# One decoder layer on one core: the first loads, the first norm, the gate rows and the planner's price for scans are changed

## The chip, the cores and the metric

The kernel runs on one core of one Trainium2 chip. The metric is the device time of one execution in microseconds, the median of several runs. The kernel before took 1553.03 us (three runs, 1550.15 to 1555.63).

## What is computed

One layer of a hybrid decoder, for a prompt of 256 tokens and 8 single-token samples together (N = 264 columns), width 2048, all in float32. Cut to what matters here:

```python
xn = rmsnorm(x, g_mix)                       # the "first norm"
z = xn @ w_in                                # RG-LRU input and gate, q, k, v, o, and 4 + 4 gate columns i, f
xr, conv_new = causal_conv(z_rgx, conv_buf, conv_w, conv_b)
r  = sigmoid(block_diag(xr, w_rg_a, b_rg_a))
ig = sigmoid(block_diag(xr, w_rg_x, b_rg_x))
log_a = -8 * r * softplus(-lam)
a  = exp(log_a)
bx = sqrt(max(1 - exp(2 * log_a), 0)) * ig * xr
h_t = a_t * h_{t-1} + bx_t                   # RG-LRU, a scan over the tokens
y_rg = rmsnorm(h * gelu(z_rgg), g_rg_out)
logi, logf = z_i + b_i, log_sigmoid(z_f + b_f)
h_ml, C, n, m = mlstm(q, k, v, logi, logf, C0, n0, m0)   # 4 heads, running maximum as stabiliser
y_ml = rmsnorm(h_ml, g_ml_out) * sigmoid(z_o)
x = x + concat(y_rg, y_ml) @ w_out
x = x + cross_attention(rmsnorm(x, g_xa), memory)
x = x + swiglu(rmsnorm(x, g_ffn))
y = rmsnorm(x, g_final)
```

The outputs are y, the recurrent states of both groups and the memory keys and values.

## The kernel before

**Layout.** The residual `xres` holds the 2048 features as 16 chunks of 128 partitions by 264 columns. Each product with a weight block of 128 by 128 is made of three fp32r products, high x high, high x low and low x high (`mm3`): ACT copies a float32 tile into a rounded high part, DVE subtracts it from the original for the low part (`split` for activations, `split_half` and `split_first` for weights). A float32 matmul that isn't split shows as two records in the profile.

**Steps.** `steps` is a list of weight pieces in order, each with its PE work and an evacuation function. A piece of 128 x 2048 feeds 48 products (16 chunks x 3) of 264 columns into one PSUM bank. Steps 0 to 3 compute the first four output blocks of `w_in` together, 4 of the 16 chunks of x in each step ("pieces" c of 512 columns, 16 in all), into four banks. Steps 4 to 7 are the other four RG-LRU input blocks, step 8 the gate columns, 9 to 16 q and k, 17 to 24 v, 25 to 32 the RG-LRU gate, 33 to 40 the mLSTM output gate, from 41 on `w_out`, then cross-attention and the feed-forward.

**Buffers.** Raw weight halves have 5 buffers, split weight halves (`w`) have 4, which is two steps' worth: the halves of step n + 2 reuse those of step n. PSUM has 4 banks `mm`, for the steps, and 4 banks `ax`, for everything else; a step's bank is the one of four steps before and has to be evacuated by then. Small temporaries `t` have 6 buffers.

**Order.** Weights are loaded on SP's queue, whose order is the order of the program text. On PE, DVE and ACT the framework's scheduler orders the instructions by priority with a timeline of its own, except inside `in_order()` (ACT and DVE) or another `manual_schedule`, where the program order holds. Once built, every engine executes its instructions strictly in the built order, and waits for what the instruction at its head needs. Work beside the steps (first norm, scans, gates, mLSTM, its norm) is written as generators (`Gen`, `side`). After each step `pump` emits pieces of them as long as the planner's clocks of DVE and ACT stay below PE's; these clocks add up prices per instruction (`price_dve`, `price_act`, `price_pe`, lines 63 to 79). A generator of negative priority is emitted whole; `finish` emits until a condition holds; `need` names what has to be finished before a step.

**Start.** Lines 1280 to 1296: SP loads chunk 0 of x, then the weight pieces 0 to 3; ACT's queue loads the first 16 columns of small vectors and chunks 1 to 3 of x. PE first runs 12 products of `ones` (`warm(12)`, line 299).

**First norm.** The products of steps 0 to 3 use x times the gain, without the norm's factor; that factor, `rstd`, is applied when a bank is evacuated. During steps 1 to 3 `sumsq` squares the chunks of x on ACT and adds them up on DVE in `acc_x`. `norm_x` (through `rstd_from`, line 343) then sums over the partitions on PE (`token_sums`: windows of 128 columns of `acc_x` as the stationary operand, one column of ones as the moving one), computes the reciprocal root on DVE, and spreads it over all partitions on PE (`spread`), from where ACT copies it to `rstd`. It is emitted after step 3 and has to be finished before step 5; the evacuation of the first four banks follows. The generator of the RG-LRU (`rg_gen`) starts at step 5 too; it has a sigmoid stage, then 16 exponentials and 8 square roots on ACT (each function set needs a table load) and 8 scans on DVE.

**Gates.** `evac_if` and `ml_gates` work on 4 partitions, one for each head, in tiles `R(j)[0:4]`. Two scans on DVE give the cumulative sums and maxima. Four products with a contraction of 4 rows spread 16 values per head over the partitions; five transposes of 4 rows turn the rows into columns. `ml_prompt` (line 661) spreads the running maximum in the same way, in one product for each head.

**What sets the order around the change.** In the sum: an ACT split of a weight half waits until PE has left that buffer two steps before; the DVE subtraction waits for ACT; whatever stands behind that subtraction in DVE's built order waits too; and PE waits for whichever of these its next instruction needs.

Of the kernel before, what the change touches and what calls it, by code (L numbers as in the profile page):

```python
# [17 lines left out]
P = 128  # L18
D = 2048
KC = D // P  # L20
T = 256
# [42 lines left out]
def price_dve(name, n, a, k):  # L64
    fast = name in ("tensor_scalar", "tensor_copy", "tensor_single_scalar", "memset")
    if name == "tensor_reduce":
        n = int(np.prod(a[1].shape[1:]))
    return 0.07 + n * (0.00052 if fast else 0.0066 if name == "reciprocal" else 0.00104)


def price_act(name, n, a, k):
# [9 lines left out]
def layer_kernel(ctx: ExitStack, tc, xT, memT, vec, wrg, w_in, w_out, w_q, w_k, w_v, w_o,  # L81
# [150 lines left out]
    def mm3(ps, a, b, start, stop):  # L232
        ah, al = a
        bh, bl = b
        pe.matmul(ps, ah, bh, start=start, stop=False)
        pe.matmul(ps, ah, bl, start=False, stop=False)
        pe.matmul(ps, al, bh, start=False, stop=stop)

    st = {}
# [53 lines left out]
    def warm(n, w=None):  # L293

        ps = bank()
        for _ in range(n):
            pe.matmul(ps[:, :P], ones if w is None else w.to_broadcast([P, P]), ones, start=True, stop=True)

    warm(12)
    onesr = const.tile([P, P], F32R, name="onesr")  # L300
    mask = const.tile([P, P], F32, name="mask")
    pool_e.affine_select(out=mask, in_=ones, pattern=[[1, P]], compare_op=OP.is_ge, fill=0.0,
# [25 lines left out]

    WIN = (0, P, N - P)

    def token_sums(ps, acc, o=0, step=1):

        for j, w0 in enumerate(WIN if acc.shape[-1] == N else WIN[:2]):
            pe.matmul(ps[:, o + j * step: o + j * step + 1], acc[:, w0: w0 + P], ones[:, 0:1],
                      start=True, stop=True)

    def spread(ps, c, n=N):

# [236 lines left out]
    def evac_if(ps):  # L575
        R = Arr(7)
        ml["R"] = R
        li, u, a, b = (R(j)[0:4] for j in range(4))
        act.activation(a, ps[64:68, :N], AF.Copy)
        act.activation(b, ps[96:100, :N], AF.Copy)  # L580
        dve.tensor_add(li, ps[0:4, :N], a)
        dve.tensor_add(u, ps[32:36, :N], b)
        dve.tensor_mul(li, li, rstd[0:4, :])
        dve.tensor_mul(u, u, rstd[0:4, :])
        dve.tensor_scalar(li, li, V("bi")[0:4], None, op0=OP.add)
        dve.tensor_scalar(u, u, V("bf")[0:4], None, op0=OP.add)
        ml["gates"] = side(ml_gates(), 1)
# [6 lines left out]
    def ml_gates():  # L594
        R = ml["R"]
        li, u, e, lf, b, g, M = (R(j)[0:4] for j in range(7))
        yield STEP
        dve.scalar_tensor_tensor(e, u, -1.0, u, op0=OP.mult, op1=OP.min)
        act.activation(e, e, AF.Exp)
        yield 0.4  # L600
        log1p(lf, e)
        yield 6.0
        dve.tensor_scalar(u, u, 0.0, None, op0=OP.min)
        dve.tensor_sub(lf, u, lf)

        one = ones[0:4, 0:1].to_broadcast([4, T])
        dve.tensor_tensor_scan(b[:, :T], one, lf[:, :T], 0.0, op0=OP.mult, op1=OP.add)
        dve.tensor_sub(g[:, :T], li[:, :T], b[:, :T])
        dve.tensor_tensor_scan(M[:, :T], g[:, :T], g[:, :T], 0.0, op0=OP.max, op1=OP.max)
        dve.tensor_add(b[:, :T], b[:, :T], M[:, :T])  # L610
        dve.tensor_scalar(M[:, :T], M[:, :T], -1.0, None, op0=OP.mult)
        dve.tensor_copy(mrow[:, 0:1], b[:, T - 1: T])

        s = slice(T, N)
        dve.tensor_add(lf[:, s], lf[:, s], V("m0", 0, 8)[0:4])
        dve.tensor_max(b[:, s], lf[:, s], li[:, s])
        dve.tensor_copy(mrow[:, 1:], b[:, s])
        x16 = e[:, 0:16]
        dve.tensor_sub(x16[:, 0:8], lf[:, s], b[:, s])
        dve.tensor_sub(x16[:, 8:16], li[:, s], b[:, s])  # L620
        act.activation(x16, x16, AF.Exp)
        pool_e.dma_start(o_m, mrow)
        yield 3.0
        yield STEP
        yield STEP
        ps = bank("ax")
        for h in range(H):
            pe.matmul(ps[:, h * 16: h * 16 + 16], ident[0:4, h: h + 1].to_broadcast([4, P]), x16,
                      start=True, stop=True)
        i4 = ident[0:4, 0:4]  # L630
        for j in range(2):
            pe.transpose(ps[:, 64 + 4 * j: 68 + 4 * j], g[:, j * P: j * P + P], i4)
        for j, w0 in enumerate(WIN):
            pe.transpose(ps[:, 72 + 4 * j: 76 + 4 * j], b[:, w0: w0 + P], i4)
        act.activation(bcs, ps[:, 0:64].rearrange("p (h j) -> p h j", j=16), AF.Copy)
        act.activation(gcol, ps[:, 64:72].rearrange("p (j h) -> p j h", h=H), AF.Copy)
        act.activation(emc, ps[:, 72:84], AF.Exp, scale=-1.0)
        yield 0.1
# [26 lines left out]
    def ml_prompt():  # L665
        qk = ml["qk"]
        yield STEP
        kt = B([P, 2, H, P])
        for tb in range(2):
            ps = bank("ax")  # L670
            for h in range(H):
                pe.transpose(ps[:, h * P: h * P + P], qk(4 + h)[:, tb * P: tb * P + P], ident)
            act.activation(kt[:, tb].rearrange("p h d -> p (h d)"), ps, AF.Copy)
            yield STEP
        while "gates" not in ml or not ml["gates"].done:
            yield STEP
        R = ml["R"]
        M = R(6)[0:4, :T]
        for h in range(H):
            sel = ident[0:4, h: h + 1].to_broadcast([4, P])  # L680
            bc = bank("ax")
            pe.matmul(bc[:, :T], sel, M, start=True, stop=True)
            sps = bank("ax")
            q, k = qk(h), qk(4 + h)
            pe.matmul(sps[:, 0:256], k[:, 0:P], q[:, 0:T], start=True, stop=True)
            pe.matmul(sps[:, 256:384], k[:, P:T], q[:, P:T], start=True, stop=True)
            w = B([P, 1024])
            E, Pm, kw = w[:, 0:384], w[:, 384:768], w[:, 768:1024]
            ml["w", h] = (Pm, kw)
            yield STEP  # L690
            dve.tensor_scalar(E[:, 0:256], bc[:, 0:T], gcol[:, 0, h: h + 1], 0.0, op0=OP.add, op1=OP.min)
            dve.tensor_scalar(E[:, 256:384], bc[:, P:T], gcol[:, 1, h: h + 1], 0.0, op0=OP.add, op1=OP.min)
            act.activation(E, E, AF.Exp)
            dve.tensor_mul(E[:, 0:128], E[:, 0:128], mask)
            dve.tensor_mul(E[:, 256:384], E[:, 256:384], mask)
            dve.tensor_mul(Pm, sps[:, 0:384], E)
            act.activation(kw[:, 0:P], kt[:, 0, h, :], AF.Copy, scale=E[:, 255:256])
            act.activation(kw[:, P:T], kt[:, 1, h, :], AF.Copy, scale=E[:, 383:384])
            yield 1.0
            ml["pn"] = h + 1  # L700
# [167 lines left out]
    def proj(src, rhs, evac, cols=2048, n=N, need=()):  # L868

        def f(i):  # L870
            ps = bank()
            w = W(i)
            nch = cols // P
            for c in range(nch):
                mm3(ps[:, :n], w(c), rhs(c), c == 0, c == nch - 1)
            return ps
        steps.append((src, cols, f, evac, need))
# [399 lines left out]
    def load_x(e, lo, hi):  # L1277
        e.dma_start(xres[:, lo:hi, :], xT[:, lo:hi, :])  # L1278

    load_x(sp, 0, 1)  # L1280
    for c in range(4):
        load_first(0, c)
    for i in range(1, 3):
        for c in range(0, 4, 2):
            load_x(sp, 4 * i + c, 4 * i + c + 2)
            load_first(i, c)
            load_first(i, c + 1)
        if i == 1:
            sp.dma_start(vecs[:, 16:], vec[:, 16:])
    with tc.high_priority(), in_order():  # L1290
        act.dma_start(vecs[:, 0:16], vec[:, 0:16])
        load_x(act, 1, 2)
        load_x(act, 2, 4)
        act.activation(warm_act, ones[:, 0:1], AF.Square)
        split_half(0, 0)
        split_half(0, 1)

    pend = []
    for i, (src, cols, pef, evf, need) in enumerate(steps):
        if i > 1:  # L1300
            load_piece(i + LD - 1)
        if i == 5:
            finish(lambda: fn.done)
            st["rg"] = side(rg_gen(), 0)
        for q in need:
            if q in st:
                finish(lambda: st[q].done)
        if i != 4:
            with tc.high_priority(300):
                for e, x in pend:  # L1310
                    e(x)
            pend = []
# [2 lines left out]
        split_half(i + LS, 0)  # L1315
        if i + LS < len(steps) and steps[i + LS][1] > 1024:
            split_half(i + LS, 1)
        ps = pef(i)
        if 1 <= i < 4:
            with tc.issue_after(st["split"].ins):  # L1320
                for c in range(4 * i if i > 1 else 0, 4 * i + 4):
                    sumsq(acc_x, xres[:, c, :], c == 0)
        if i == 3:
            fn = side(norm_x(), -1)
        if evf is not None:
            pend.append((evf, ps))
        if i == 0:
# [124 lines left out]
```

## Time and profile before

| | |
|---|---|
| runs | 1550.15, 1553.03, 1555.63 us |
| the profiled execution | span 1548.1 us; it has no other time of its own |
| TensorE clock granted | 0.997 on average |
| instructions of PE | 12098 |
| read from memory | 312.78 MB, 209 GB/s over the span |
| chain that ended last | PE 96%, DVE 2%, ACT 1% |

A row of a timeline has the start and the length in us, engine, line, operation, tiles (output <- inputs, buffer numbers left out), shapes and count, and in brackets the idle time before it and who ended it. Line 60 is the wrapper through which all priced engine calls go, so tiles tell the calls apart: `mm` and `ax` are PSUM banks, `raw` and `w` weight halves before and after the split, `B` large tiles, `c` and `t` small ones. PEld is the loading of the stationary operand. In the chain of waits a row is start, length and what ran. A row of waits is: who waited for whom, us in total, times, longest. A row of windows has the window, its length, the busy time of PE, PEld, DVE, ACT and POOL with counts, the granted clock, the DMA share and GB/s.

### The profile page before, as it was taken

The numbers are of one execution on the slowest core, as the hardware profiler recorded it, in microseconds if no ns is written. First come the engines' busy times: TensorE is split into PE (matmuls) and PEld (weight loads), VectorE is DVE, ScalarE is ACT, GpSimd is POOL, SyncE is SP. The second block draws the span as 40 slices with busy tenths as digits, with TensorE's granted clock in tenths as the row PEclk, the third lists the DMA queues.
The fourth block names the chain that finished last, engine by engine and source line by source line (L and its number), as shares of the span: only waits on it lengthen the run. The fifth ranks groups of instructions, "written<-read, shape, count | busy, mean of one in ns | idle before, by whom it ended". The sixth has DMA issues, their size and how long they took to land.

```text
span 1548.1 us, 30188 instructions
## 1 busy us (share of the span) xinstructions
PE 1533.5 (99%) x12098; PEld 1500.4 (97%) x12098; DVE 1055.5 (68%) x2026; ACT 784.0 (51%) x1255; POOL 123.7 (8%) x190
## 2 busy tenths in 40 slices
PE   9999999999999999999999999999999999999997
PEld 9999999999999888899999999999999999999997
DVE  7886888796699989876665555445555545555554
ACT  7565775665455656555444444333444433444463
POOL 0001210000134333310000000000000000000000
PEclk9999999999999999999999999999999999999999
DMA  9556984547789887855555555555555555555563
GB/s 301 187 164 204 309 288 171 193 158 259 251 294 356 320 296 252 309 181 180 187 177 181 186 181 188 181 185 183 183 185 181 186 183 186 180 188 178 163 181 107
DMA packets 99757, 326.01 MB, mean 211 GB/s; under 512 B 10945, under 2 KB 19825, under 8 KB 99617
## 3 DMA queue, kind: packets, MB, share of 16 engines
q1 hardware_dynamic: 83472, 269.57, 52.1%
q0 software_dynamic: 15136, 53.16, 9.7%
q8 instruction: 94, 1.54, 0.4%
q10 hardware_dynamic: 1008, 1.36, 0.3%
q14 instruction: 47, 0.38, 0.1%
HBM read 312.78 MB, written 11.28 MB: 209 GB/s over the span
## 4 chain that ended last, share of the span: by engine, by line
PE 96%; DVE 2%; ACT 1%; DMA 0%; issue 0%; SPq 0%; DVEq 0%; ACTq 0%
PE mm L60 90%; PE ax L60 6%; DVE B L60 1%; ACT B L60 0%; DVE w L60 0%; DMA raw<-w_in 0%; ACT w L60 0%; ACT L60 0%; DVE xres L60 0%; DVE c L60 0%; ACT rstd L60 0%; SPq L1278 0%; DVE acc_x L60 0%; DVEq L1429 0%; ACT t L60 0%
## 5 line engine op out<-in xcount | busy, mean ns | idle before, releaser
L60 PE MATMUL mm<-B,w 128*128 128x264 f32 (+1 forms) x10960 | 1365.3, 285 | 4.1 <-DVE w L60 2.4
L60 PEld LDWEIGHTS mm<-B,w 128*128 128x128 f32 x10960 | 1338.6, 188 | 16.4 <-DVE w L60 2.8
L60 ACT ACTIVATE w<-raw 128x1024 fp32r<-128x1024 f32 (+1 forms) x522 | 537.9, 1031 | 654.6 <-PE mm L60 447.3
L60 DVE TENSOR_TENSOR w<-raw,w 128x1024 fp32r<-128x1024 f32 (+1 forms) x522 | 623.1, 1195 | 357.0 <-ACT w L60 356.0
L60 PE MATMUL mm<-w,B 128*128 128x512 f32 x384 | 91.0, 391 | 0.0
L60 PEld LDWEIGHTS mm<-w,B 128*128 128x128 f32 x384 | 70.7, 188 | 14.3
L60 DVE TENSOR_TENSOR t<-mm,rstd 128x264 f32<-128x264 f32 x104 | 44.8, 431 | 44.2 <-PE mm L60 43.5
L1344 POOL TENSOR_TENSOR B<-B,rstd 128x264 f32<-128x264 f32 x4 | 2.8, 736 | 855.5 <-ACT rstd L60 855.5
L60 DVE TENSOR_TENSOR xres<-xres,mm 128x264 f32<-128x264 f32 (+1 forms) x81 | 34.2, 423 | 38.9 <-PE mm L60 38.9
L60 DVE SCALAR_TENSOR_TENSOR B<-B,dw 128x256 f32<-128x256 f32 x128 | 55.6, 488 | 3.9 <-ACT dw L60 3.9
L60 DVE SCALAR_TENSOR_TENSOR dw<-B,qsm,dw 128x256 f32<-128x256 f32 x96 | 49.6, 525 | 0.4
L60 PE MATMUL ax<-B,B 128*128 128x256 f32 (+3 forms) x288 | 48.1, 308 | 0.0
L60 PEld LDWEIGHTS ax<-B,B 128*128 128x128 f32 x288 | 40.8, 190 | 3.2 <-ACT w L60 0.3
L1031 POOL TENSOR_TENSOR ds<-dw,ds 128x256 fp32r<-128x256 f32 x32 | 34.6, 1085 | 108.1 <-ACT ds L60 108.1
L60 ACT ACTIVATE B<-xres,vecs 128x264 fp32r<-128x264 f32 (+1 forms) x64 | 32.1, 502 | 1.5 <-DVE xres L60 1.0
L60 ACT ACTIVATE t<-xres 128x264 f32<-128x264 f32 (+2 forms) x61 | 24.0, 410 | 15.2 <-DVE xres L60 15.2
L1020 POOL DMA_DIRECT2D B<-kcT x32 | 17.3, 542 | 140.1 <-DVE B L60 131.0
L60 ACT ACTIVATE B<-t 128x264 fp32r<-128x264 f32 (+1 forms) x60 | 24.2, 409 | 4.6 <-DVE t L60 4.3
L60 DVE TENSOR_TENSOR acc_x<-acc_x,t 128x264 f32<-128x264 f32 x59 | 25.1, 426 | 1.0 <-ACT t L60 0.5
L60 DVE SCALAR_TENSOR_TENSOR B<-xres,vecs,B 128x264 fp32r<-128x264 f32 x48 | 23.4, 487 | 3.1 <-ACT B L60 3.1
L60 ACT ACTIVATE t<-t 128x264 f32<-128x264 f32 (+1 forms) x61 | 24.8, 406 | 1.3 <-DVE t L60 1.2
L60 ACT ACTIVATE dw<-B,qsm 128x256 f32<-128x256 f32 x32 | 16.2, 507 | 17.4 <-DVE B L60 10.7
(152 smaller groups left out, 666.9 us busy)
## 6 DMA issues: line engine op xcount, KB each, us to landing
raw<-w_gu SPq DMA_DIRECT2D x176, 512.0 KB, 3.5
raw<-w_d SPq DMA_DIRECT2D x80, 512.0 KB, 3.5
raw<-w_in SPq DMA_DIRECT2D x74, 512.0 KB, 4.6
raw<-w_out SPq DMA_DIRECT2D x32, 512.0 KB, 4.0
B<-kcT POOLq DMA_DIRECT2D x32, 512.0 KB, 8.1
raw<-w_q SPq DMA_DIRECT2D x32, 512.0 KB, 3.7
B<-vcT POOLq DMA_DIRECT2D x32, 512.0 KB, 8.5
raw<-w_k SPq DMA_DIRECT2D x32, 512.0 KB, 6.8
```

The source lines that it names most:

```text
L60: return f(*a, **k)
L1020: pool_e.dma_start(kc, kcT[h, b])
L1031: pool_e.tensor_sub(ws[:, 1], acc, ws[:, 0].bitcast(F32))
L1344: e.tensor_mul(st["y"](c), st["y"](c), r)
```

## The change

Loads: SP now issues weight piece 0 first, then chunk 1 of x, piece 1, chunks 2 and 3, pieces 2 and 3; ACT's queue issues chunk 0 of x and then the vectors. The warm-up has 8 products. The squares of chunks 8 to 11 are emitted with those of 12 to 15, after step 3. The two PE stages of the first norm are emitted at chunk 2 of steps 5 and 6, and from step 4 to 6 PE's order is the program's. The evacuation of steps 3 to 6 and the RG-LRU's generator are emitted at step 7. The gate rows' products contract over all 128 partitions, of which POOL sets the unused ones to zero, and the transposes become products with columns of the identity. `token_sums` streams 128 columns of ones for each window; only the first column of each result is used. The planner's price for a scan is doubled.

```diff
@@ price_dve
-    return 0.07 + n * (0.00052 if fast else 0.0066 if name == "reciprocal" else 0.00104)
+    rate = {"reciprocal": 0.0066, "tensor_tensor_scan": 0.0021}.get(name, 0.00052 if fast else 0.00104)
+    return 0.07 + n * rate
...
-    warm(12)
+    warm(8)
@@ token_sums
-    def token_sums(ps, acc, o=0, step=1):
+    def token_sums(ps, acc, o=0):
         for j, w0 in enumerate(WIN if acc.shape[-1] == N else WIN[:2]):
-            pe.matmul(ps[:, o + j * step: o + j * step + 1], acc[:, w0: w0 + P], ones[:, 0:1],
-                      start=True, stop=True)
+            pe.matmul(ps[:, o + j: o + j + P], acc[:, w0: w0 + P], ones, start=True, stop=True,
+                      skip_group_check=True)
@@ evac_if
         ml["R"] = R
+        for q in range(2):
+            pool_e.memset(R.tile(q), 0.0)
@@ ml_gates
-            pe.matmul(ps[:, h * 16: h * 16 + 16], ident[0:4, h: h + 1].to_broadcast([4, P]), x16,
+            pe.matmul(ps[:, h * 16: h * 16 + 16], ident[:, h: h + 1].to_broadcast([P, P]), R(2)[:, 0:16],
                       start=True, stop=True)
-        i4 = ident[0:4, 0:4]
-        for j in range(2):
-            pe.transpose(ps[:, 64 + 4 * j: 68 + 4 * j], g[:, j * P: j * P + P], i4)
-        for j, w0 in enumerate(WIN):
-            pe.transpose(ps[:, 72 + 4 * j: 76 + 4 * j], b[:, w0: w0 + P], i4)
+        for o, x, at in ((64, R(5), WIN[:2]), (72, R(4), WIN)):
+            for j, w0 in enumerate(at):
+                pe.matmul(ps[:, o + 4 * j: o + 4 * j + 4], x[:, w0: w0 + P], ident[:, 0:4], start=True, stop=True)
@@ ml_prompt
-        M = R(6)[0:4, :T]
+        M = R(6)[:, :T]
         for h in range(H):
-            sel = ident[0:4, h: h + 1].to_broadcast([4, P])
+            sel = ident[:, h: h + 1].to_broadcast([P, P])
@@ proj
             for c in range(nch):
+                if i in (5, 6) and c == 2:
+                    with tc.high_priority():
+                        st["rstd_x"].run(lambda: True)
                 mm3(ps[:, :n], w(c), rhs(c), c == 0, c == nch - 1)
@@ the loads
-    load_x(sp, 0, 1)
     for c in range(4):
         load_first(0, c)
+        if c == 0:
+            load_x(sp, 1, 2)
+        elif c == 1:
+            load_x(sp, 2, 4)
...
     with tc.high_priority(), in_order():
+        load_x(act, 0, 1)
         act.dma_start(vecs[:, 0:16], vec[:, 0:16])
-        load_x(act, 1, 2)
-        load_x(act, 2, 4)
@@ the loop over steps
-        if i == 5:
-            finish(lambda: fn.done)
+        if i == 7:
             st["rg"] = side(rg_gen(), 0)
...
-        if i != 4:
+        if not 4 <= i < 7:
             with tc.high_priority(300):
                 for e, x in pend:
                     e(x)
...
+        if i == 4:
+            kept.enter_context(tc.manual_schedule(engines={mybir.EngineType.PE}))
         ps = pef(i)
-        if 1 <= i < 4:
+        if i == 6:
+            kept.close()
+        if i in (1, 3):
             with tc.issue_after(st["split"].ins):
-                for c in range(4 * i if i > 1 else 0, 4 * i + 4):
+                for c in range(8 if i == 3 else 0, 16 if i == 3 else 8):
                     sumsq(acc_x, xres[:, c, :], c == 0)
         if i == 3:
-            fn = side(norm_x(), -1)
+            st["rstd_x"] = Gen(norm_x())
```

More of the change, by code (lines that the diff above doesn't have):

```diff
@@ L1298, in layer_kernel @@
     pend = []
+    kept = ExitStack()
     for i, (src, cols, pef, evf, need) in enumerate(steps):
```

## The prediction

> **What bounds the kernel now.** I read the page's first lines, then the idle time of TensorE (PE), then the chain of waits and the timeline at the places where PE idles. Rows that stand between those shown are left out.
>
> ```profile
> span 1548.1 us, 30188 instructions
> PE 1533.5 (99%) x12098; PEld 1500.4 (97%) x12098; DVE 1055.5 (68%) x2026; ACT 784.0 (51%) x1255; POOL 123.7 (8%) x190
> ```
>
> ```profile
> PE mm L60 <- DVE w L60: 2.4, 2, 1.5
> PE mm L60 <- DVE B L60: 1.7, 1, 1.7
> PE mm L60 <- DVE ones L60: 1.1, 1, 1.1
> PE ax L60 <- ACT w L60: 0.7, 1, 0.7
> ```
>
> PE is the bound: a microsecond of PE idleness is a microsecond of time, and little is left to win: 1.1 + 0.7 us before the first real product, 1.7 us after the first norm, 1.5 us in the scan stretch (the other 0.9 us of the DVE w row comes much later, where the order is unchanged). I compared the instruction order of both built programs, engine by engine; it says what each PE instruction waits for and what stands before it. From the mixer's output projection on, the order is the same but for names.
>
> **Start.** The first piece of weights moves ahead of the first x tile on SP; x and the small vectors go to ACT's queue; the warm-up shrinks from 12 to 8 products.
>
> ```profile
> 0.81 0.39 SPq L1278 DMA_DIRECT2D xres<-xT  x1
> 1.12 5.38 PE L60 MATMUL mm<-ones 128*128 128x128 f32 x24 [1.12 <-DVE ones L60]
> 3.62 0.50 ACT L60 ACTIVATE B<-xres,vecs 128x264 fp32r<-128x264 f32 x1
> 6.50 0.63 ACT L60 ACTIVATE w<-raw 128x512 fp32r<-128x512 f32 x1 [2.38 <-DMA raw<-w_in]
> 7.18 0.99 PE L60 MATMUL ax<-B,w 128*128 128x264 f32 x6 [0.67 <-ACT w L60]
> 15.21 0.63 ACT L60 ACTIVATE w<-raw 128x512 fp32r<-128x512 f32 x1 [0.30 <-DMA raw<-w_in]
> ```
>
> ```profile
> raw<-w_in SPq DMA_DIRECT2D x8, 256.0 KB, 5.2
> xres<-xT SPq DMA_DIRECT2D x1, 132.0 KB, 2.2
> ```
>
> ```profile
> 0.00:3.80 3.80, 2.67 (x12) 2.68 (x13) 0.17 (x1) 1.57 (x3) 0.94 (x7) 1.00 0.47 105
> ```
>
> The last number of the window row is GB/s: 105 over 3.8 us are 399 KB. In the new order 256 + 132 + 8 KB (the vectors) stand up to the end of the first piece, so it lands near 3.9 us; ACT splits it at about 4.2, PE follows 0.68 later (6.50 to 7.18), at 4.9. That is 2.3 us earlier. ACT's own first operand needs x tile 0 and the vectors, as at 3.62, and those two only change queues. If the piece takes the 5.2 us of its row from an issue at 0.81, it lands at 6.0 and PE starts at 6.75. I take 4.9: the 132 KB transfer at the queue's head landed in 2.2.
>
> A warm-up record lasts 5.38/24 = 0.22 us; the same shape later takes 0.10 (the spread below: 6 records, 0.58, two of its three products 128 columns wide), so the array ran at half clock through the warm-up, though the clock column says 1.00, and came up about when it ended; I take 6.3. Eight products end at 1.12 + 16 x 0.22 = 4.7. Real products between 4.9 and 6.3 then run at half speed and lose 0.7. Start: **-1.6** (bounds -2.2; +1.3, with a landing at 6.0 and half clock for 3.4 us after it). The later pieces come at about their old times: that of piece 8 (of 16) came by DMA at 15.21, and PE, 1.46 us a piece, reached it at 7.18 + 8 x 1.46 = 18.9; 1.6 less still hides it. Two x transfers moved from ACT's queue into SP's put the issue of pieces 1 to 3 back by two issues of some 0.4 us (the first row); piece 1 hides behind PE's 1.46 us, or twice that at half clock, on piece 0.
>
> **First norm at fixed places, squares later.** Steps are weight pieces of 48 products.
>
> ```profile
> 30.65 9.36 PE mm L60 x78
> 40.02 0.56 PE ax L60 x6
> 48.23 0.58 PE ax L60 x6
> ```
>
> ```profile
> 19.70 2.03 DVE L60 TENSOR_TENSOR acc_x<-acc_x,t 128x264 f32<-128x264 f32 x4
> 36.08 0.38 DVE L60 TENSOR_TENSOR acc_x<-acc_x,t 128x264 f32<-128x264 f32 x1
> 36.81 1.06 ACT L60 ACTIVATE w<-raw 128x1024 fp32r<-128x1024 f32 x1 [2.02 <-PE mm L60]
> 37.91 1.22 DVE L60 TENSOR_TENSOR w<-raw,w 128x1024 fp32r<-128x1024 f32 x1 [1.17 <-ACT w L60]
> 39.05 0.16 DVE L60 TENSOR_SCALAR t<-t 128x8 f32<-128x8 f32 x1
> 51.12 1.10 PE L60 MATMUL mm<-B,w 128*128 128x264 f32 x7 [1.73 <-DVE B L60]
> ```
>
> Step 4 starts at 30.65; at 9.36/78 = 0.12 a product it ends at 36.41. The last square was added at 36.08, before the split of step 6's second half (ACT 36.81, DVE 37.91), which waits for step 4's buffer, so for the end of step 4. In the changed order the last two additions stand *behind* that DVE subtraction, and the sums on PE stand behind only six products of step 5. So PE runs 0.72 us past the end of step 4 and waits. The chain from the end of step 4: ACT at +0.40, DVE at +1.50, next instruction +2.64 (39.05), a reciprocal, the two additions 0.53 apart (2.03 for four), the last done at about +3.7, sums at +3.8: **3.1 us of idleness where there was none**. Behind it stand all products of PE. Then 0.6 for the sums, 42 products (5.04), 6 more (0.72), the spread (0.58) and 42 (5.04): step 7 starts at +15.8. It started at 51.12, +14.7: there the wait of 1.73 us goes away, because rstd now comes 5 us before the bank is needed. Net **+1.1** (bounds 0.9, 1.4).
>
> **Gate rows and scans.**
>
> ```profile
> 101.83 1.06 ACT L60 ACTIVATE w<-raw 128x1024 fp32r<-128x1024 f32 x1 [1.82 <-PE mm L60]
> 103.64 1.28 ACT L60 ACT_TABLE_LOAD   x1
> 104.94 2.96 ACT L60 ACTIVATE B<-B,rgc 128x264 f32<-128x264 f32 x7
> 116.97 0.61 PE L60 MATMUL ax<-B,ident 4*128 4x16 f32 x4
> 119.18 0.81 PE L60 MATMUL ax<-ident,B 4*128 4x4 f32 x5
> 120.27 1.20 DVE L60 TENSOR_TENSOR w<-raw,w 128x1024 fp32r<-128x1024 f32 x1
> 121.52 9.76 PE L60 MATMUL mm<-B,w 128*128 128x264 f32 x66 [1.53 <-DVE w L60]
> ```
>
> From the split at 101.83 ACT runs sigmoids, a table load, 16 exponentials, a second load and the square roots; DVE's scans follow, and the split of step 17's second half stands behind them: PE resumes at 121.52, 19.7 us later. The changed order has the same block behind the split that waits for step 16 and ending at step 19, with one more table load inside (1.30, from 103.64 to 104.94) and one exponential fewer: 21.0 us. The nine gate products no longer fill PE's wait; they now run ahead of step 16, where they cost their own time, 1.75 us of the 3.05 between 116.97 and 120.0 (four products of 264 columns take 0.5, four transposes 0.8). Four more transposes fill instead (-0.8). Net +1.3 + 1.75 - 0.8 = **+2.2** (1.5 to 2.6: the lower if 128 rows run at 0.1 a record). The 128 rows also need two memsets on POOL, which had nothing else to do there. The doubled scan price is a number in the planner; it moved this block, as the later start of the recurrence's side work did (and its two weight loads on SP, needed only there).
>
> **An evacuation falls behind.** This is the largest term, at step 34, near 230 us. PE may begin step 34 only when DVE has emptied the bank of step 30. In the changed order that instruction (t<-mm,rstd) stands behind the subtraction of the second half of step 35, whose ACT part waits for the end of step 33, the PE instruction just before. Between the two stand five instructions of the sample recurrence.
>
> ```profile
> 215.13 0.29 DVE L60 SCALAR_TENSOR_TENSOR t<-B,B 128x128 f32<-128x128 f32 x1
> 215.25 1.06 ACT L60 ACTIVATE w<-raw 128x1024 fp32r<-128x1024 f32 x1 [1.23 <-PE mm L60]
> 215.35 0.43 DVE L60 TENSOR_TENSOR t<-mm,rstd 128x264 f32<-128x264 f32 x1
> 216.35 1.23 DVE L60 TENSOR_TENSOR w<-raw,w 128x1024 fp32r<-128x1024 f32 x1 [0.36 <-ACT w L60]
> ```
>
> ACT begins 0.4 after PE's end (36.41 to 36.81), DVE 1.1 later, its next instruction 1.14 later: 2.6. The five recurrence instructions take 1.9 (0.5 after each long one, 0.2 to 0.3 after each short one, as at 215.13 and 215.35), the evacuation 0.43: **+4.9** (4.3 without gaps in the triples, 5.5 with a pause at each). Before, such evacuations stand ahead of the split, as at 215.35, and PE has no idle row there.
>
> **Clock.**
>
> ```profile
> 51.00:55.00 4.00, 3.88 (x32) 3.91 (x33) 4.00 (x12) 1.22 (x5) 0.00 (x0) 1.00 0.37 137
> 122.00:126.00 4.00, 4.00 (x23) 4.00 (x22) 4.00 (x6) 0.61 (x2) 0.00 (x0) 0.57 0.59 180
> ```
>
> The third number from the end is the granted clock. After small products and 1.53 us of idleness it fell to a mean of 0.57 over 4 us: 0.43 x 4 = 1.7 us lost. After 1.73 us of plain idleness at 51 it stayed at 1.00. The new block idles some 4 us, so its drop stays. The 4.9 us at step 34 should cost another **+1.6** (0 to 1.7). The 3.1 us at the sums lies between the two cases: **+0.8** (0 to 1.7). The page "TensorE: Matmul & The Clock Gate" of the Trainium skill, section "What's actually happening", has the clock halved after an idle window of about 3.4 us. By that alone the sums' wait would cost nothing, and the sum would be 0.8 less; the drop at 122 us, after 1.53 us of idleness among small products, doesn't bear out so high a limit.
>
> **Sums over 128 columns.** Six records took 0.56 with one column and 0.58 in the spread, mostly 128 columns. 26 such products: **+0.2** (0 to 1.0, if 0.04 each).
>
> Sum: -1.6 + 1.1 + 2.2 + 4.9 + 1.6 + 0.8 + 0.2 = +9.2: a span of 1557.3. The span of 1548.1 lies 4.9 below the median of the runs, 1553.0; I keep that: 1562.2.
>
> **Rivals.**
> *The clock holds.* The waits come, but no drop follows, also not in the scan stretch, since the gate products now use 128 rows: -2.2 + 1.1 + 1.5 + 4.3 - 1.7 = +3.0, 1556.0. For it: no drop at 51 us. Against it: idle stretches three times that long.
> *The first piece is no earlier*, and every term is at its upper bound: 1.3 + 1.4 + 2.6 + 5.5 + 1.7 + 1.7 + 1.0 = +15.2, 1568.2. For it: the 5.2 us landing.
> *The splits run ahead* (faster). All three new waits hang on one mechanism: ACT cannot split a half before PE has left the buffer two steps back. Were ACT free of that wait, at the sums, the scans and step 34 alike, no wait would be left: -1.6 - 1.7 - 1.5 - 1.7 (clock) = -6.5, 1546.5. It decides from a buffer freed 3 us, half a step, earlier. Against it: the split at 36.81 waited 2.02 us for PE, the one at 215.25 1.23.
>
> **How the numbers follow.** Forecast 0.66, clock holds 0.15, first piece late 0.12, splits ahead 0.07. Within 0.3% (4.7 us, what a measurement of this kernel can tell) lies only the second: faster 0.07, same 0.15, slower 0.78. The range goes from the second rival's place to just below the third's: 1556.5 to 1567.5.
>
> **What would show it.** The first real product near 4.9; an idle row of about 3 us before the sums near 38, released by the last addition to acc_x; no wait at step 7; idle rows near 130 released by DVE w; one near 230, 4 to 5 us long, released by t<-mm; a clock of 0.5 behind it. Without that last wait the forecast is wrong by half its size.

## The result and the profile after

| | before | after |
|---|---|---|
| median of four runs each, on one chip | 1551.74 us | 1559.51 us |
| lowest and highest | 1550.15 to 1555.63 | 1558.39 to 1560.54 |
| span of the profiled execution | 1548.1 | 1558.7 |
| granted clock, mean | 0.997 | 0.992 |

The ratio is 1.0048, 95% interval 1.0034 to 1.0062: slower by half a per cent. First the page's own lines and the view of waits of PE in the changed kernel (us in total, times, longest).

```profile
span 1558.7 us, 30195 instructions
...
PE 1536.8 (99%) x12095; PEld 1505.0 (97%) x12095; DVE 1058.0 (68%) x2026; ACT 795.0 (51%) x1263; POOL 125.1 (8%) x192
```

```profile
PE mm L60 <- DVE t L60: 4.6, 1, 4.6
PE ax L60 <- DVE acc_x L60: 2.7, 1, 2.7
PE mm L60 <- DVE w L60: 2.2, 2, 1.4
PE mm L60 <- ACT w L60: 1.2, 1, 1.2
...
PE ax L60 <- DVE B L60: 1.1, 1, 1.1
```

Against the rows of before, the 1.7 us at step 7 (mm <- DVE B) are gone. Two rows are new, 4.6 and 2.7. The scan stretch now has three waits (1.4 of the DVE w row, 1.2, 1.1) in place of one of 1.5. From the timeline of the changed kernel, first the start:

```profile
1.12 3.78 PE L60 MATMUL mm<-ones 128*128 128x128 f32 x16 [1.12 <-DVE ones L60]
...
4.29 0.51 ACT L60 ACTIVATE B<-xres,vecs 128x264 fp32r<-128x264 f32 x1 [1.09 <-DMA vecs<-vec]
...
4.71 0.61 ACT L60 ACTIVATE w<-raw 128x512 fp32r<-128x512 f32 x1
...
5.37 1.33 PE L60 MATMUL ax<-B,w 128*128 128x264 f32 x6 [0.47 <-ACT w L60]
...
6.33 0.63 ACT L60 ACTIVATE w<-raw 128x512 fp32r<-128x512 f32 x1 [0.61 <-DMA raw<-w_in]
```

The first real product starts at 5.37. The weight piece held nobody up (the row at 4.71 has no wait); the small vectors did, which ACT got at 4.29. The second piece came 0.61 late for ACT. The first norm, same view:

```profile
35.52 1.06 ACT L60 ACTIVATE w<-raw 128x1024 fp32r<-128x1024 f32 x1 [0.74 <-PE mm L60]
...
36.78 1.22 DVE L60 TENSOR_TENSOR w<-raw,w 128x1024 fp32r<-128x1024 f32 x1
...
38.45 0.43 DVE L60 TENSOR_TENSOR acc_x<-acc_x,t 128x264 f32<-128x264 f32 x1
...
38.93 0.94 PE L60 MATMUL ax<-ones,acc_x 128*128 128x128 f32 x6 [2.73 <-DVE acc_x L60]
...
60.63 1.06 ACT L60 ACTIVATE w<-raw 128x1024 fp32r<-128x1024 f32 x1 [0.74 <-ACT B L60]
```

The split at 35.52 waits for the end of step 4. Its counterpart before, at 36.81, waited a little longer: for PE's 242nd weight product, two of step 5 included, where this one waits for the 240th. Counted by PE's own weight products (the 241st starts at 35.32 in place of 36.37), PE is 1.05 us ahead there. The subtraction at 36.78 follows it, the last addition stands behind, PE waits 2.73 us. The split at 60.63 is, counted from the start, the same one as this row of before:

```profile
59.12 1.06 ACT L60 ACTIVATE w<-raw 128x1024 fp32r<-128x1024 f32 x1 [0.85 <-PE mm L60]
```

PE's weight products are 1.5 us late here too. So 1.05 us ahead have become 1.5 behind: the first norm cost 2.6 us net, with the wait at step 7 already taken off. The scan stretch:

```profile
116.85 1.06 ACT L60 ACTIVATE w<-raw 128x1024 fp32r<-128x1024 f32 x1 [1.76 <-PE mm L60]
...
133.57 0.52 PE L60 MATMUL mm<-B,w 128*128 128x264 f32 x2 [1.25 <-ACT w L60]
...
135.47 0.59 PE L60 MATMUL ax<-ident,B 128*128 128x128 f32 x3 [1.06 <-DVE B L60]
...
137.91 3.45 PE L60 MATMUL mm<-B,w 128*128 128x264 f32 x14 [1.41 <-DVE w L60]
```

From the split that waits for PE to the last of the three waits it is 21.1 us, with three table loads of ACT inside (at 117.93, 120.10 and 128.97). Step 34 in the timeline of the changed kernel:

```profile
241.74 1.06 ACT L60 ACTIVATE w<-raw 128x1024 fp32r<-128x1024 f32 x1 [1.23 <-PE mm L60]
...
242.83 1.22 DVE L60 TENSOR_TENSOR w<-raw,w 128x1024 fp32r<-128x1024 f32 x1 [0.58 <-ACT w L60]
...
245.77 0.43 DVE L60 TENSOR_TENSOR t<-mm,rstd 128x264 f32<-128x264 f32 x1
...
246.34 7.94 PE L60 MATMUL mm<-B,w 128*128 128x264 f32 x43 [4.64 <-DVE t L60]
```

The split, its subtraction, five instructions of the recurrence between 243.97 and 245.77, the evacuation, and only then PE. Last, windows of PE alone (window, length, PE's busy time with count, granted clock, DMA share, GB/s), cut where the clock changed:

```profile
36.86:40.27 3.41, 1.34 (x11) 1.00 0.91 271
40.27:43.69 3.42, 3.42 (x18) 0.50 0.56 207
43.69:47.10 3.41, 3.41 (x30) 1.00 0.09 18
132.43:135.84 3.41, 1.21 (x9) 1.00 0.00 0
135.84:139.25 3.41, 2.00 (x10) 0.50 0.06 24
139.25:142.67 3.42, 3.42 (x17) 0.50 0.72 218
241.66:245.07 3.41, 0.04 (x1) 1.00 0.82 280
245.07:248.49 3.42, 2.15 (x10) 0.50 0.75 189
248.49:251.90 3.41, 3.41 (x17) 0.50 0.22 90
```

The clock is either 1.00 or 0.50, and it changes only on a grid of 3.41 us: 40.27 to 135.84 are 28 such periods, to 245.07 another 32. A period in which PE did little is followed by one at half clock, however PE works by then. The loss is half the busy time in the periods at 0.50: 1.7 us behind the sums, 1.0 + 1.7 in the scan stretch (1.7 before), 1.1 + 1.7 behind step 34. The Trainium skill, page "TensorE: Matmul & The Clock Gate", section "What's actually happening", has the window at 3413 ns, free-running; the length agrees with these windows, and the grid's place does differ between executions (last section).

### The profile page after: what moved, and what is told of

Read it like the earlier page. It is cut to its first block, busy times and chain, and to the rows that moved or that the text cites. A ratio compares the mean times of both kernels' runs of the same rounds, so it can differ in the third digit from the quotient of the medians.

```text
span 1558.7 us, 30195 instructions
## 1 busy us (share of the span) xinstructions
PE 1536.8 (99%) x12095; PEld 1505.0 (97%) x12095; DVE 1058.0 (68%) x2026; ACT 795.0 (51%) x1263; POOL 125.1 (8%) x192
## 4 chain that ended last, share of the span: by engine, by line
PE 94%; DVE 2%; ACT 2%; DMA 1%; issue 1%; SPq 0%; DVEq 0%; ACTq 0%
PE mm L60 89%; PE ax L60 5%; DVE B L60 1%; DMA raw<-w_in 1%; ACT w L60 1%; ACT B L60 1%; DVE w L60 0%; ACT t L60 0%; ACT L60 0%; SPq L200 0%; DVE acc_x L60 0%; SPq L1282 0%; DVE t L60 0%; DVE xres L60 0%; DVE c L60 0%
```

## The experiments

Each time is the median of 5 to 12 runs; ratios are to the kernel before on the same chip, with 95% intervals.

### The norm's edit alone, and everything but it

Kernel `norm_only` is the kernel before with these parts of the change, and `no_norm` is the changed kernel with the same parts taken back:

```diff
+                if i in (5, 6) and c == 2:
+                    with tc.high_priority():
+                        st["rstd_x"].run(lambda: True)
...
-        if i == 5:
-            finish(lambda: fn.done)
+        if i == 7:
             st["rg"] = side(rg_gen(), 0)
...
-        if i != 4:
+        if not 4 <= i < 7:
...
-        if 1 <= i < 4:
+        if i in (1, 3):
...
-            fn = side(norm_x(), -1)
+            st["rstd_x"] = Gen(norm_x())
```

> The kernel before with the norm's edit alone: squares in two groups, sums and spread at fixed places, the recurrence's side work from step 7. Start, gate rows, scan price and width of the sums are as before. Theory: the waits at the sums, in the scan stretch and at step 34 all come from this edit. PE idles 2.4 to 2.7 us before the sums, some 3.7 us in the scan stretch and 3 to 4.6 us near 230, released by t<-mm; against the changed kernel only the earlier start (1.3) is missing, and the wait near 230 may be a little shorter: 1557 to 1562 us. Rival: the doubled scan price and the gate rows put the evacuation behind the split, so there is no wait near 230 (less 4.6 and 2.8 of clock): 1553 to 1555 us.

> The changed kernel with the norm's part taken back: sums and spread where side work puts them, squares after each piece, the recurrence from step 5; start, gate rows, scan price and 128 columns stay. Theory: these four are worth little together: start -1.3, some 1 us more of idleness in the scan stretch (the scan price moves its block), 0.2 at the sums, no idle row before the sums near 38, one of some 1.8 at step 7, none over 1 us near 230: 1551 to 1553 us. Rival: the scan price or the gate rows alone put an evacuation behind a split; then there is an idle row of 3 us or more between 205 and 250 and the time is 1555 or more.

`norm_only`: 1560.76 us, ratio 1.0057 (1.0042 to 1.0072). `no_norm`: 1553.95, 1.0020 (1.0011 to 1.0029). The view of waits of `norm_only`:

```profile
PE mm L60 <- DVE t L60: 3.6, 1, 3.6
...
PE ax L60 <- DVE acc_x L60: 2.0, 1, 2.0
PE mm L60 <- ACT w L60: 1.2, 1, 1.2
```

The norm's edit alone makes the whole loss, and all three kinds of waits, the late evacuation too; by the count of weight products it stands one step earlier here, at step 33. The other four parts together are slower by 0.2%, 1 us above the expected range; no wait of 3 us is in their trace, so the rival falls too. The two losses, 9.1 and 2.3 us by the medians, add up to more than the 7.8 of the whole change: the parts act on one order, and their effects can't simply be summed.

### One other part at a time

`start_only`, `gates_only` and `price_only` are the kernel before with one part each; `single_price` is the changed kernel with that one line taken back:

```diff
-    rate = {"reciprocal": 0.0066, "tensor_tensor_scan": 0.0021}.get(name, 0.00052 if fast else 0.00104)
+    rate = {"reciprocal": 0.0066}.get(name, 0.00052 if fast else 0.00104)
```

> The kernel before with the new order of the first loads and the warm-up of 8 alone. Theory: the start is worth what it was worth by the end of step 4 in the changed kernel, 1.3 us, and no engine after it is at its limit, so all of it stays: first real product near 5.4, 1551.7 - 1.3 = 1550.4 us (1549.8 to 1551). Rival: PE, ahead by 1.3 us, waits for the recurrence between 150 and 200, as the kernel with the late sums did, and loses it there: 1551.7 us, with idle rows of about 1 us near 190.

> The kernel before with the gate rows on 128 partitions alone. Theory: the clock falls where PE has little to do for a few us, whatever the number of rows of its small products; the stretch of half clock near 122 stays and the time with it: 1551.6 us (1551 to 1552.3). Rival: products over four partitions are what lets the clock fall; with 128 it stays at 1.00 near 122 and 1.7 us are won: 1549.9 us.

> The kernel before with the scans priced double in the planner alone. Theory: it makes some of the 2.3 us by which the changed kernel without the norm's part is slower than the kernel before: the scan block moves by a few rows, an evacuation near 213 falls behind (0.5 to 1 us), and a wait on the recurrence near 185: 1552.5 to 1554 us. Rival: the price alone changes nothing, and the wider sums or gate rows make that loss: 1551.6 us.

> The changed kernel with the scans priced once in the planner, as before. Theory: the price only decides which evacuation falls behind which split. Another one is late, by 3.6 us as in the kernel with the norm's edit alone, in place of 4.6; everything else stays: 1557 to 1558.7 us, an idle row of some 3.6 us near 230, released by t<-mm. Rival: the doubled price is what puts it there; with it gone the row goes and 7.4 us with it: 1552 us.

| kernel | us | ratio | 95% |
|---|---|---|---|
| `start_only` | 1552.13 | 1.0004 | 0.9995 to 1.0013 |
| `gates_only` | 1551.92 | 1.0000 | 0.9990 to 1.0011 |
| `price_only` | 1553.43 | 1.0012 | 1.0002 to 1.0021 |
| `single_price` | 1558.63 | 1.0047 | 1.0034 to 1.0059 |

*The start* is worth nothing that shows when it stands alone; both the theory's 1.3 us and the place that the rival named were wrong. Its timeline:

```profile
6.94 0.63 ACT L60 ACTIVATE w<-raw 128x512 fp32r<-128x512 f32 x1 [1.32 <-DMA raw<-w_in]
...
18.45 0.63 ACT L60 ACTIVATE w<-raw 128x512 fp32r<-128x512 f32 x1 [0.91 <-DVE B L60]
...
30.48 2.69 PE L60 MATMUL mm<-B,w 128*128 128x264 f32 x20 [0.47 <-DVE w L60]
```

The second piece comes 1.32 us late for ACT (0.61 in the changed kernel). A later piece is split at 18.45, where ACT did it at 17.42 before; from there ACT has no pause until 33, and at 30.48 PE waits for a split weight half. PE's lead, 1.9 us at the first real product, is 1.0 after the second piece and 0.2 behind this wait (the split that waits for the end of step 4 began at 36.59, against 36.81). In `no_norm`, where the three engines have the same order up to there, that later piece is split at 17.57 and 1.1 us of lead are left. So the lead differs between executions with the times at which pieces come.

*The price* makes much of the loss of `no_norm`, as expected: 1.4 us by the medians, with an interval that only just leaves out no change, and 1.7 by the waits of its trace, 1.0 near 186 and 0.7 near 228, which `no_norm` has too (1.6 and 0.7). In the changed kernel it matters little: without it PE waits 3.6 us in place of 4.6 (mm <- DVE t), as in `norm_only`, and the median is 0.9 lower, within the runs' spread. There it decides which evacuation falls behind, not whether one does.

*The gate rows* change nothing, as expected, and the clock falls near 122 as it did (from 123.55 here). But this execution has two drops that the profile of before had not. Windows of `gates_only`, and the PE row of its timeline in the one from 225.95:

```profile
48.46:51.87 3.41, 1.67 (x15) 1.00 0.48 163
51.87:55.28 3.41, 3.41 (x18) 0.50 0.45 154
...
225.95:229.37 3.42, 3.42 (x33) 1.00 0.80 248
229.37:232.78 3.41, 3.41 (x18) 0.50 1.01 406
```

```profile
226.51 2.74 PE L60 MATMUL ax<-ones,B 128*128 128x1 f32 x24
```

PE is busy through the whole period from 225.95, with 24 records that stream one column each, and the clock falls all the same. `price_only` lost two periods behind such sums, from 237.30 to 244.13; the three other profiles with narrow sums there lost none. In the changed kernel, where these sums stream 128 columns, no drop follows them in its profile, nor in any of the eight others with the wide sums. And the wait of 1.7 us at step 7, which cost no clock in the profile of before, did here (48.46 to 55.28).

### The sums later

```diff
-                if i in (5, 6) and c == 2:
+                if (i, c) in ((5, 10), (6, 8)):
```

> The changed kernel with the sums after ten chunks of step 5 in place of two, and the spread after eight chunks of step 6. Theory: the 2.7 us before the sums are pure lateness of the last addition; 24 products more in front cover them, and with the idleness the stretch of half clock behind it (1.7 us) goes: 1559.5 - 4.4 = 1555.1 us (1554.5 to 1556). No idle row near 39, the clock 1.00 from 36 to 44, rstd still in time for step 7. Rival 1: the wait moves to step 7, 1.7 us as in the kernel before: 1556.8 us, with an idle row there released by DVE B. Rival 2: the clock falls there whatever PE does: 1556.8 us, without such a row, clock 0.5 behind 40.

1559.10 us, ratio 1.0042 (1.0028 to 1.0056): 0.4 less than the changed kernel, not 4.4. In the profiled execution (span 1555.3, 3.4 less) the local part came as expected: no idle row at the sums or at step 7, the clock 1.00 there. PE was still 4.6 us ahead of the changed kernel where it begins a group of mLSTM products (183.14 against 187.71). Then, at the next group of the same kind, in its timeline:

```profile
193.47 0.59 PE L60 MATMUL ax<-B,ident 128*128 128x256 f32 x2
...
197.25 1.14 PE L60 MATMUL ax<-B,B 128*128 128x258 f32 x4 [1.23 <-DVE B L60]
198.23 0.72 PE L60 MATMUL ax<-ones,B 128*128 128x1 f32 x6
```

The six products at 198.23 stand at 200.65 in the changed kernel: half the lead is lost, 1.23 us of it in the wait shown for DVE's part of the mLSTM, which was not ready sooner. So none of the three expectations held. That execution was also the fastest of its five, and the profiled one of the changed kernel among its slower ones, so the 3.4 flatters the edit; what keeps the others slower was in no trace.

### The wait at the sums filled

```diff
+                if i == 5 and c == 2:
+                    fill = bank("ax")
+                    for _ in range(11):
+                        pe.matmul(fill[:, :P], ones, ones, start=True, stop=True)
                 if i in (5, 6) and c == 2:
```

> The changed kernel with eleven products of ones by ones, read by nobody, ahead of the sums on PE, in the place where it idles. They take 11 x 0.22 = 2.4 us of the 2.7, so nothing comes later. Theory: the half clock from 40.3 to 43.7 follows from PE's idleness before the sums; with the gap filled the clock stays at 1.00 there and 1.7 us are saved: 1557.8 us (1557.3 to 1558.3), an idle row of 0.3 us or none. Rival: the clock falls for another reason (the small sums, the transfers): 1559.5 us, with clock 0.5 behind 40.

1558.97 us, ratio 1.0049 (1.0033 to 1.0064); by the time alone nothing is decided. The timeline, and one window:

```profile
36.08 2.62 PE L60 MATMUL ax<-ones 128*128 128x128 f32 x22
38.90 0.91 PE L60 MATMUL ax<-ones,acc_x 128*128 128x128 f32 x6 [0.20 <-DVE t L60]
```

```profile
40.00:44.00 4.00, 4.00 (x36) 1.00 0.37 141
```

The sums come at 38.90 as in the changed kernel (38.93), and the clock stays at 1.00 behind them. That fits the theory, but one trace doesn't settle it: the next kernel kept its clock there without any filling.

### Another ring for the gate evacuations

```diff
-            z = tmp()
+            z = ltmp()
             dve.tensor_mul(z, ps[:, :N], rstd)
```

> The changed kernel with the evacuation t<-mm,rstd of the recurrence's gate steps taken from the ring lt in place of t. Theory: the evacuation of step 30 stands behind the split of step 35 because its buffer of the ring t is still held by the sample recurrence; with a buffer of its own it comes ahead, the 4.6 us at step 34 go and with them 2.8 us of lowered clock: 1559.5 - 7.4 = 1552.1 us (1551.3 to 1553), no idle row between 150 and 340. Rival 1: the planned order, not the buffer, holds it back: 1559.5 us, with the idle row still there. Rival 2: the wait moves on to the sums of the norms near 254: about half comes back, 1555 to 1557 us.

The ring `lt` has 3 buffers; some norm and mLSTM rows use it too, the five recurrence instructions don't. 1552.38 us, ratio 1.0002 (0.9992 to 1.0011), where 1552.1 was expected: 7.1 us gone by one word. The timeline has no idle row at step 34 any more:

```profile
229.72 14.53 PE L60 MATMUL mm<-B,w 128*128 128x264 f32 x120
```

Nothing but the ring was edited, so it was the buffer. And the same wait before the sums, here 2.74 us, cost no clock in this execution:

```profile
34.80:38.21 3.41, 1.54 (x13) 1.00 0.95 339
38.21:41.62 3.41, 2.53 (x21) 1.00 0.72 243
41.62:45.04 3.42, 3.42 (x31) 1.00 0.30 122
```

Here the idle stretch lies across the border of two periods, and each kept enough products. In the changed kernel most of it lay in one.

### Both cures, a later recurrence, and the start again

`ring_and_late` has the two edits above; `combined` has them and the recurrence's side work from step 8, as shown here; `combined_old_start` is `combined` with the loads and the warm-up of before:

```diff
-        if i == 7:
+        if i == 8:
             st["rg"] = side(rg_gen(), 0)
```

> The changed kernel with the ring lt for the gate evacuations, the sums after ten chunks of step 5, the spread after eight of step 6, and the recurrence's side work from step 8. Theory: no idle row at the sums, at step 7 and at step 34; left are one of 1.2 to 1.9 us in the scan stretch with 1.7 us of lowered clock, and some 1 us near 185, where PE, now ahead, waits for the recurrence on DVE. Against the kernel before: start -1.3, step 7 -1.7, the wait near 185 +1, the rest even: 1549 to 1551 us, faster than both kernels. Rival: the recurrence on DVE and ACT paces the stretch from 150 to 200, and what is won ahead of it is lost there: 1551.7 us or more, with idle rows of 2 us or more in all between 180 and 200.

> The changed kernel with both cures, the ring lt for the gate evacuations and the later sums, the recurrence's side work still from step 7. Theory: the combined kernel was 5 us faster than the kernel before because no wait is left that is long enough to lower the clock, and these two cures do that; starting the recurrence a step later adds little: 1546.5 to 1549 us, no idle row at 39 and 230. Rival: two thirds of what the later sums win are lost between 150 and 200, as in the kernel with them alone, and the later recurrence is what avoids that: 1550 to 1551 us, idle rows of 2 us or more in all between 180 and 200.

> The combined kernel with the old order of the first loads and the old warm-up of 12. Theory: the new start is worth 1.2 us once the squares come later (the combined kernel is ahead by 1.21 at the end of step 4), though alone it left 0.2: 1546.4 + 1.2 = 1547.6 us (1547 to 1548.3). Rival: the start is worth nothing at the end here either: 1546 to 1546.8 us.

| kernel | us | ratio | 95% |
|---|---|---|---|
| `ring_and_late` | 1548.70 | 0.9978 | 0.9969 to 0.9986 |
| `combined` | 1546.43 | 0.9967 | 0.9955 to 0.9980 |
| `combined_old_start` | 1547.41 | 0.9972 | 0.9961 to 0.9983 |

All three are faster than both kernels. One of the seven runs of `combined_old_start` took 8532 us, for a reason that no trace here shows; without it the median is 1547.1. `combined` is so by 5 us, 2.6 below the expected range, which had counted on one poor period in the scan stretch and a wait near 185; neither is there in its profile. In `ring_and_late` the later sums are worth 3.7 us on top of the ring, and nothing is given back near 190. In `combined` the scan stretch still has idleness; windows on the grid show what became of the clock:

```profile
130.97:134.38 3.41, 2.65 (x23) 1.00 0.42 147
134.38:137.79 3.41, 2.78 (x23) 1.00 0.00 0
137.79:141.20 3.41, 2.04 (x17) 1.00 0.30 88
141.20:144.61 3.41, 3.41 (x31) 1.00 0.68 241
```

The idleness is broken up, no period is poor enough, and from the start to 1537 us the clock stays at 1.00 (in the last 6 to 9 us it is at 0.50 in every kernel). `ring_and_late` lost two periods there, from 132.85 to 139.68. The start, by the two medians, is worth 1.0 us in `combined` (0.7 without the long run, 1.4 by the two spans); the intervals overlap, so the times alone don't show it. The traces do: with the squares later, PE's lead of 1.4 us at step 7 is still 1.4 at the last weight product.

## Why the prediction was right

The sum was +9.2 on the span of 1548.1; measured it is +10.6. The forecast of 1562.2 was 2.7 above the median, because two errors ran against each other: the terms were 1.4 too low, and the offset from span to median 4.1 too high (4.9, where 0.8 was measured). That the terms came so near is in part luck too, since the start and the clock cost more than was put down, the gate rows and the evacuation less.

*Start, -1.6: about -1.1.* The first real product came 1.8 us earlier, not 2.3. The step that failed there is "those two only change queues": the vectors now stand second on ACT's queue and came at 4.29, while the operand that needs them began at 3.62 before. The weight piece was in time, as predicted. By the grid (40.27 less ten periods) the full clock came at 6.14, so products ran at half speed for 0.8 us, which cost 0.3 of the lead. The rest went later: "the later pieces come at about their old times" failed for the piece that ACT split at 18.84 (17.42 before), behind which PE lost another 0.3.

*First norm, +1.1, and its clock, +0.8: +2.6 together.* The wait was 2.73 where 3.1 was forecast, at the place, by the chain and with the releaser named; the one at step 7 went. The missing 0.4 is in part a misreading: the 0.4 us from the end of step 4 to ACT's split held two products of step 5, 0.24 us. The clock took 1.7 of the 2.6 in this execution.

*Gate rows and scans, +2.2: about 1.7, the clock's part included.* It is what is left of 10.6 after 1.5 up to the split at 60.63 and 7.4 at step 34. The block came out as counted: 21.1 us from the split at 116.85 to 137.91, where 21.0 was forecast, with the one more table load. Of the three idle rows one was released by DVE w, as forecast, the others by ACT w and DVE B. The idleness went from 1.5 to 3.7 us and the clock cost 1.0 more; the four transposes of the forecast run between these waits (eight records from 131.94 to 135.77), and what else made up for the difference is not shown.

*The evacuation, +4.9: 4.64.* Mechanism, place, releaser and size were right, and `own_ring` shows that the buffer is the cause. What the prediction left open was which edit puts it there. It is the norm's: `norm_only` has a late evacuation of 3.6 us, `no_norm` one of 0.7 alone. The price, which it named as one mover, brings those 0.7 by itself (`price_only`) and with the norm's edit only chooses among evacuations.

*Clock, +2.4 beyond what it cost before: about 5.5.* This term was mis-sized. The prediction let the length of a wait decide. What decides is how much PE streams in a period of 3.41 us, and a poor one costs up to 1.7, a long wait two of them: 1.7 at the sums, 1.0 more in the scan stretch, 2.8 at step 34.

*Sums over 128 columns, +0.2.* The price holds: a row of 24 such records takes 2.84 us in `single_price`, where 24 of one column take 2.74 in `gates_only`. What was missed is the gain, the drop that narrow sums can bring (`gates_only`).

*The offset, 4.9: 1.8 in the changed kernel* (1560.46 for the execution whose span is 1558.7). With the same 1.8 the profiled execution of before, which had one poor period, took 1549.9, at the lower end of its runs; that of the changed kernel was among its slower ones. So the profile's difference, 10.6, is larger than that of the medians, 7.8.

The rival "the clock holds" fell with the first window at 0.50; "the first piece is no earlier" fell at 4.71; and "the splits run ahead" fell with the split at 35.52, which waited for PE again.

## What to carry to other kernels

Moving one stage by a step or two can put an evacuation behind a split far downstream, where no line was edited: after such a move, look for buffers whose last user now stands behind a wait on PE, and give that evacuation a ring that the side work doesn't use. Price a wait by more than its length: add the clock, which goes by how much PE streams in each period, and break up idleness rather than gather it (`combined`; that filling it helps was seen in one trace and not in the time). One profiled execution is one draw of the clock's grid, so compare medians before a term of a microsecond or two is believed.

## What the runs showed of the hardware that was not expected

The clock's rule can be read closely. In all fourteen profiles (before, after, twelve kernels) I counted, for each period of the grid in the first 300 us, the columns that PE streamed: a weight product counts its 264, a record of a product with unsplit float32 operands twice its columns, since such records follow each other after 0.22 us for 264 columns where weight products do after 0.12. Products across a border were shared out by time. Of some 1,200 periods 33 were followed by half clock, all with up to about 2,900 columns; every one from about 3,030 on was followed by full clock, at full and at half speed alike. About 7,500 fit into a period (3.41 / 0.12 x 264), so the line lies near 40%. It is not known more closely: counted by the products' starts alone, two periods with full clock behind them have 2,850 and 2,900. The wait of 2.7 us at the sums falls on either side of it by chance (2,800 in the changed kernel, 3,030 in `own_ring`), and the grid's place differs between executions: full clock began at 6.14 in the changed kernel and at 4.08 in `own_ring` (34.80 less nine periods). Four or 128 partitions in the gate rows made no difference to the drop near 122 (`gates_only`); the number of columns does: the one-column sums of `gates_only` keep PE "busy" for a whole period and count as next to nothing. The same page of the Trainium skill, section "HAM oscillation — how this bites in real kernels", gives the rule as no idle gaps above about 3.4 us; here 2.73 us were enough, and in `gates_only` no gap at all.
